# A two-layer mixer trunk: the order of projection tiles in a stage, and the evacuation of rotary tiles

## The chip, the cores and the metric

The kernel runs on one core of a Trainium2 chip. TensorE (PE in the profile) multiplies matrices into PSUM; VectorE (DVE), ScalarE (ACT) and GpSimd (POOL) do the elementwise work, and SyncE (SP) issues the DMAs. The metric is the device time of one execution in microseconds, as the median of several runs.

## The reference, cut to what matters

Two layers of a decoder trunk over 1024 positions with 1024 channels, and one final RMSNorm. Each layer normalizes x, projects it with one wide matrix, feeds three causal mixers, gates and merges their outputs, projects back and adds to x:

```python
h = rms_norm(x, norm_g) * (1.0 + scale) + shift
proj = h @ w_in
pool_u, pool_g, q, k, v, ret_g, rw, rw_g, gate_logits = jnp.split(proj, points, axis=-1)
o_pool = causal_pool_mixer(pool_u, pool_w, pool_scale) * jax.nn.silu(pool_g)
o_ret = retention(q, k, v, positions, ret_norm_g) * jax.nn.silu(ret_g)
o_rwkv = rwkv7_time_mix(rw, shift_mu, ...) * jax.nn.silu(rw_g)
branches = jnp.stack([o_pool, o_ret, o_rwkv], axis=2)
y = jnp.einsum('btnw,nwd->btnd', branches, w_branch)
merged = jnp.sum(jax.nn.sigmoid(gate_logits) * y, axis=2)
return x + gate * (merged @ w_out)
```

Retention turns q and k by position before it uses them:

```python
x1, x2 = x32[..., :half], x32[..., half:]
return jnp.concatenate([x1 * cos - x2 * sin, x1 * sin + x2 * cos], axis=-1)
```

The RWKV mixer is a recurrence over time with a state of 64x64 per head; it is the one part that cannot run over all positions at once.

## The kernel before

**Tiles.** Activations lie with channels on the 128 partitions and positions along the free axis, in two halves of 512. A projection tile is 128 output channels. Each of its two halves is accumulated over 8 blocks of input channels, with three products per block (high and low parts of weight and activation), so 48 matmuls of 128x512 for a tile. `in_tile2` (L1362) takes two of the three PSUM banks of the pool `psa` for the halves of a tile and runs half the channels into the first bank, half into the second, and then the other halves. The next tile's first half can start in the third bank; its second half needs the bank of this tile's first half, which must have been evacuated by then.

**Stages.** The work of a layer is in four stages, one for each retention head and each pair of RWKV heads. `RW(h)` (L55) stands for the three tiles k, r, v of RWKV, `RT(h)` for the four retention tiles rq, rk, rv, rg, `PL(g)` for the two pooling tiles pu, pg, and gate tiles serve as filler. `plan_layer` (L415) hands out the order, tile by tile and one ahead of the tile that runs. It looks at `prog`, the progress of the RWKV task: when that task of the current stage has reached its inversion (`prog` at 0 or more), the stage's retention tiles come, and then k, r, v of the next stage.

**Evacuation.** `evac_steps` (L1011) takes a tile out of PSUM. k, r and v go through `shift_evac` (L963): a scaled copy on ACT, and one product and sum on DVE. rq and rk go through `rotary` (L980): the table for this half, cosines over partitions 0 to 63 and sines over 64 to 127, is loaded from DRAM each time; four DVE products over 64 partitions each, and a sum on POOL. rv and pu take a copy on ACT, rg and pg a tanh on ACT and a product on DVE, a gate tile a tanh on ACT alone. A gate tile that is made early goes to DRAM and is loaded again for the merge.

**Tasks.** Work that is not projection is written as generators in five lanes ("norm", "post", "rwkv", "mix", "ada"). `pump` (L362) advances each lane after every projection matmul, by due times on the planner's own clock, and only the head of a lane runs. `evac_steps` adds `rwkv_task` (L725) when v is done, and `ret_task` (L655) or `pool_task` (L593) to "mix" when rg or pg is done. `rwkv_task` has a preparation (scans, exponentials, transposes, Gram matrices; its last DVE product is bv, L834), an inversion of small triangular blocks on DVE (L842 to L867), and 16 chunks one after another (L908). Both `ret_task` and the preparation pass their products through the two PSUM banks of tag `mx`. Retention's q, k, v and gate and pooling's inputs share eight SBUF slots (`mi`).

**Order within an engine.** The code's order is a priority; the tile framework then sets the order of each engine's instructions ahead of time, so an instruction that is ready early can stand ahead of one written before it. At run time each engine goes through its list in that order.

Of the kernel before, what the change touches and what calls it, by code (L numbers as in the profile page):

```python
# [9 lines left out]
F32 = mybir.dt.float32  # L10
# [3 lines left out]
ALU = mybir.AluOpType  # L14
# [3 lines left out]
P = 128  # L18
# [4 lines left out]
HF = 512  # L23
# [31 lines left out]
def RW(h):  # L55
    return [("k", h), ("r", h), ("v", h)]


def RT(h):
    return [("rq", h), ("rk", h), ("rv", h), ("rg", h)]  # L60


def PL(g):
    return [("pu", g), ("pg", g)]


def GT(n, *ds):
    return [("gate", n, d) for d in ds]


def BR(n, *ds):
    return [("br", n, d) for d in ds]
# [17 lines left out]
def trunk_kernel(ctx, tc, xT, cvec, pos, vecs, consts, w_ada, w_all, pool_w, lora_w, out):  # L90
    nc = tc.nc
# [10 lines left out]
    dp = ctx.enter_context(tc.tile_pool(name="dp", bufs=1, space=DRAM))  # L102
# [4 lines left out]
    def nm(s):  # L107
        uid[0] += 1
        return f"{s}_{uid[0]}"

    def slot(tag, n, w=HF):
        def f(s, dt=F32):
            return tp.tile([P, w], dt, tag=tag, name=nm(s), bufs=n)

        return f
# [4 lines left out]
    t_mi = slot("mi", 8, HF + 16)  # L120
    t_mo = slot("mo", 4, HF + 16)
    t_vp = slot("vp", 2)
    t_cs = slot("cs", 2)
    mi = lambda s: t_mi(s)[:, 0:HF]
    mo = lambda s: t_mo(s)[:, 0:HF]

# [22 lines left out]
    def cs(k, n=None):  # L149
        o = CST[k]  # L150
        return cst[:, o : o + n] if n else cst[:, o : o + 1]
# [85 lines left out]
    def run(gen):  # L237
        for _ in gen:
            pass

    rope_d = dp.tile([2, P, HF], F32, name="rope_d")

    def rope_tables():
        yield 15000
        MAGIC = 12582912.0
        TWO_PI = 2.0 * math.pi
        cw, left = [], TWO_PI
        for _ in range(3):
            e = 2.0 ** (math.frexp(left)[1] - 8)
            cw.append(math.floor(left / e) * e)  # L250
            left -= cw[-1]
        cw.append(left)
        PI_F = 3.1415925
        for h in range(2):
            s = slice(h * HF, (h + 1) * HF)
            pi = t_mo("posi", I32)[:, 0:HF]
            tc.keep_in_program_order(nc.sync.dma_start(out=pi, in_=pos[:, s].to_broadcast([P, HF])))
            ang = mo("ang")
            nc.vector.tensor_copy(ang, pi)
            nc.vector.tensor_scalar_mul(ang, ang, cs("freq"))  # L260
            n = mo("nrot")
            for big in (4096.0, 1.0):
                nc.vector.tensor_scalar(n, ang, 1.0 / (TWO_PI * big), MAGIC, op0=ALU.mult, op1=ALU.add)
                nc.vector.tensor_scalar_sub(n, n, MAGIC)
                for cc in cw:
                    nc.vector.scalar_tensor_tensor(ang, n, -cc * big, ang, op0=ALU.mult, op1=ALU.add)
                yield 6000
            m = mo("over")
            nc.vector.tensor_scalar_add(n, ang, math.pi / 2)
            nc.vector.tensor_scalar(m, n, math.pi, -TWO_PI, op0=ALU.is_gt, op1=ALU.mult)  # L270
            nc.vector.tensor_tensor(n, n, m, op=ALU.add)
            for a in (n, ang):
                nc.vector.tensor_scalar(a, a, PI_F, -PI_F, op0=ALU.min, op1=ALU.max)
            nc.scalar.activation(n[0:64, :], n[0:64, :], AF.Sin)
            nc.scalar.activation(n[64:128, :], ang[64:128, :], AF.Sin)
            nc.sync.dma_start(out=rope_d[h], in_=n)
            yield 6000

    xd = [dp.tile([8, 2, P, HF], F32, name=f"xd{l}") for l in range(1)]
# [4 lines left out]
    lanes = {k: deque() for k in names}  # L284
# [115 lines left out]
    prog = {}  # L400
    early = [set() for _ in range(L)]
# [4 lines left out]
    def out_order(l, part):  # L406
        return (2, 3, 0, 4, 5, 1, 6, 7) if kept(l) and part else range(8)
# [3 lines left out]
    def plan():  # L411
        for l in range(L):
            yield from ((l, it) for it in plan_layer(l))

    def plan_layer(l):  # L415
        yield from [("lora",)] + RW(0)
        pools = deque(PL(i) for i in range(4))
        pre = deque(GT(0, *range(8)) + GT(1, 0, 1, 4, 5, 6, 7) + GT(2, 2, 3, 4, 5, 6, 7, 0, 1) + GT(1, 2, 3))
        late = deque([("wg", 0), ("wg", 1), ("wg", 2)])
        done = 0  # L420
        while done < 4 or prog.get((l, 3), 0) < 13 or pools:
            if done < 4 and prog.get((l, done), -1) >= 0:
                yield from RT(done)
                done += 1
                if done < 4:
                    yield from RW(done)
            elif pools and 4 - len(pools) <= done and len(lanes["mix"]) < 2:
                yield from pools.popleft()
            elif pre or late:
                q = late if late and (done == 4 and prog.get((l, 3), -1) >= 0 or not pre) else pre  # L430
                it = q.popleft()
                early[l].add(it)
                yield it
            elif pools:
                yield from pools.popleft()
            elif done < 4:
                yield from RT(done)
                done += 1
                if done < 4:
                    yield from RW(done)  # L440
            else:
                break
        yield ("merge",)
        seq = GT(1, 2, 3) + BR(0, 0, 2, 4, 6) + [("wg", 0), ("wg", 1)]
        seq += GT(1, 0, 1) + BR(1, 0, 2) + GT(1, 4, 5) + BR(1, 4)
        seq += [("wg", 2), ("wg", 3)] + GT(1, 6, 7) + BR(1, 6)
        seq += GT(2, 0, 1) + BR(2, 0) + GT(2, 2, 3) + BR(2, 2) + GT(2, 4, 5, 6, 7) + BR(2, 4, 6)
        yield from [it for it in seq if it not in early[l]]
        for part in range(2 + (l + 1 == L)):
            yield from [("out", d, part) for d in out_order(l, part)]  # L450
# [41 lines left out]
    def mm1(ps, w, k, r, start, stop):  # L492
        (whi, wlo), (rh, rl) = w, r
        for j, (a, b) in enumerate(((whi, rh), (whi, rl), (wlo, rh))):
            mmul(ps, a[:, k * P : (k + 1) * P], b, start=(start and j == 0), stop=(stop and j == 2))
            pump()
# [5 lines left out]
    def acc_ps():  # L502
        return ps_a.tile([P, HF], F32, tag="acc", name=nm("acc"))
# [459 lines left out]
    def shift_evac(l, mui, ps, h, am_prev, dst):  # L963
# [13 lines left out]
        )  # L977
        return carry

    def rotary(ps, h, dst):  # L980
        cs_ = t_cs("cs")
        nc.sync.dma_start(out=cs_, in_=rope_d[h])
        cos, sin = cs_[0:64, :], cs_[64:128, :]
        lo, hi = ps[0:64, :], ps[64:128, :]
        t = mo("rot")
        nc.vector.tensor_tensor(dst[0:64, :], lo, cos, op=ALU.mult)
        nc.vector.tensor_tensor(dst[64:128, :], hi, cos, op=ALU.mult)
        nc.vector.scalar_tensor_tensor(t[0:64, :], hi, -1.0, sin, op0=ALU.mult, op1=ALU.mult)
        nc.vector.tensor_tensor(t[64:128, :], lo, sin, op=ALU.mult)  # L989
        nc.gpsimd.tensor_tensor(dst, dst, t, op=ALU.add)  # L990

    L_ = None
    pinned = [False]

    def enter_layer(l):
        nonlocal L_
        L_ = (l, {}, {}, [])
        L_[3].extend(lora_load(l))

    def lora_load(l):  # L1000
        raw = wp.tile([P, W], F32, tag="wr", name=nm("lraw"), bufs=3)
        nc.sync.dma_start(out=raw, in_=lora_w[l])
        lw = [cp.tile([P, W], F32R, tag=f"lw{j}", name=nm("lw")) for j in range(2)]
        split(raw, *lw, nc.vector)
        return lw
# [5 lines left out]
    def evac_steps(item, ps, h, bias=None):  # L1011
        l, st, ams, lw = L_
        kind = item[0]
# [65 lines left out]
    def evac(*a):  # L1079
        run(evac_steps(*a))  # L1080
# [137 lines left out]
    with tc.manual_schedule(engines={ET.PE, ET.DVE, ET.Activation, ET.Pool}):  # L1218
# [107 lines left out]
        for kt in range(8):  # L1326
            shifted(1, kt)
            mm1(pss[0, 1], first[0][1][kt // 4], kt % 4, h_cur[1][kt], kt == 0, kt == 7)
        L_ = (0, {}, {}, [])
        evac(first[0][0], pss[0, 0], 0)  # L1330
# [10 lines left out]
    run(sb)  # L1341
    L_[3].extend(lora_load(0))
    wprep()
    evac(first[0][0], pss[0, 1], 1)
    for h in range(2):
        evac(first[1][0], pss[1, h], h)
    setup_rest()
    add("mix", rope_tables())
    late_ada = [(0, g) for g in (5, 6)] + [(1, g) for g in range(7)]

    for l in range(L):
        if l:
            enter_layer(l)
# [91 lines left out]
        while wready[0][0][0] != "out":  # L1445
# [6 lines left out]
            elif it[0] == "gate":  # L1452
                n, d = it[1], it[2]
                for h, ps in enumerate(in_tile2(ws)):
                    nc.scalar.activation(gate_tile((n, d, h)), ps, AF.Tanh, scale=0.5)
            else:
                n, d0 = it[1], it[2]
# [5 lines left out]
                for d, h in dh:  # L1463
                    ps = acc_ps()
# [29 lines left out]
        for part, (h, sl) in enumerate(parts):  # L1494
# [3 lines left out]
            for i, d in enumerate(out_order(l, part)):  # L1498
# [16 lines left out]
                ps = acc_ps()[:, 0 : xr.free_size()]  # L1515
# [129 lines left out]
```

## Time and profile before

| | |
|---|---|
| median of 3 runs | 2549.88 us (2545.69 to 2555.64) |
| the profiled execution | 2560.67 us, span 2558.9 us |
| busy: PE, DVE, ACT, POOL | 95%, 55%, 31%, 33% |
| mean granted TensorE clock | 0.968 |
| table loads for rotary | 32, of 256 KB each |
| early gate halves written to DRAM | 72 |

A row of a timeline has start and length in microseconds, the engine, the line, the operation, what it writes and reads, and in brackets how long the engine sat idle before it and what ended that. A row of a group has busy time and the mean of one in ns, and then the idle time before them with its releasers. A row of windows has the window, the busy time of PE, weight loads, DVE, ACT and POOL with counts, the granted TensorE clock as a share, and the DMA share and rate. A tensor's name in such rows is that of the code, without its buffer number.

### The profile page before, as it was taken

Reading aid. Unit: us, or ns where it says so; the run is one execution under the profiler, and the core shown is the slowest. Engines: PE = TensorE matmul, PEld = TensorE weight load, DVE = VectorE, ACT = ScalarE, POOL = GpSimd, SP = SyncE. Lnnn points to the kernel's source line nnn. Section 1 sums busy time; section 2 is a strip of 40 time slices with the busy share of each in tenths; the row PEclk is TensorE's granted clock in tenths of the full one; section 3 lists DMA queues with packets and bytes.
Section 4 is the critical chain, followed back from the end, with each engine's and each line's share of the span. In section 5 each row is a group of like instructions: output and inputs, shape, how many; then the busy total and the mean of one; then the engine's idle time right before and its main releaser. Section 6 shows DMA issues by size and latency. Waiting matters only on the chain. (4 is left out here: it accounts for less than half of the span.)

```text
span 2558.9 us, 34979 instructions
## 1 busy us (share of the span) xinstructions
PE 2420.1 (95%) x13318; PEld 2000.1 (78%) x13318; DVE 1415.3 (55%) x2620; ACT 800.7 (31%) x1482; POOL 850.3 (33%) x729
## 2 busy tenths in 40 slices
PE   6888999999999899999999899999999989999998
PEld 4677887787787688777878788778778778878888
DVE  7887358257646834365464835744764583412244
ACT  4641332233133222212353223323313322222243
POOL 5422232133223223473452223223322322247341
PEclk8799999799999999999999999999999999999999
DMA  6222112112212314674540211211221121454152
GB/s 227 76 86 77 41 43 78 42 43 68 65 39 70 120 46 138 208 225 129 173 133 26 82 43 51 77 48 42 66 67 39 46 78 42 144 169 123 56 156 75
DMA packets 126329, 227.62 MB, mean 89 GB/s; under 512 B 14288, under 2 KB 17616, under 8 KB 126160
## 3 DMA queue, kind: packets, MB, share of 16 engines
q1 hardware_dynamic: 126160, 225.37, 28.2%
q8 instruction: 105, 1.72, 0.3%
q14 instruction: 64, 0.52, 0.1%
HBM read 180.75 MB, written 44.56 MB: 88 GB/s over the span
## 5 line engine op out<-in xcount | busy, mean ns | idle before, releaser
L392 PE MATMUL acc<-hhi,wh 128*128 128x512 f32 x1968 | 801.2, 407 | 53.6 <-DVE rot L989 52.0
L507 POOL TENSOR_TENSOR wl<-wr,wh 128x512 fp32r<-128x512 f32 x338 | 448.8, 1329 | 1171.9 <-ACT wh L506 1059.0
L392 PE MATMUL acc<-hlo,wh 128*128 128x512 f32 x1968 | 801.2, 407 | 0.0
L392 PE MATMUL acc<-hhi,wl 128*128 128x512 f32 x1968 | 800.8, 407 | 0.0
L392 PEld LDWEIGHTS acc<-hhi,wh 128*128 128x128 f32 x1968 | 378.1, 192 | 125.4 <-issue 55.3
L506 ACT CAST wh<-wr 128x512 fp32r<-128x512 f32 x338 | 209.4, 620 | 835.9 <-PE acc L392 658.7
L392 PEld LDWEIGHTS acc<-hlo,wh 128*128 128x128 f32 x1968 | 378.2, 192 | 73.1 <-issue 5.0
L392 PEld LDWEIGHTS acc<-hhi,wl 128*128 128x128 f32 x1968 | 377.8, 192 | 69.5 <-issue 1.1
L392 PE MATMUL acc<-olo,wh 128*128 128x512 f32 x384 | 154.7, 403 | 3.7 <-POOL olo L507 3.7
L392 PE MATMUL acc<-oG,wh 128*128 128x512 f32 x384 | 153.5, 401 | 3.1 <-DVE gs L1472 1.3
L392 PE MATMUL acc<-oG,wl 128*128 128x512 f32 x384 | 153.1, 400 | 0.0
L930 DVE SCALAR_TENSOR_TENSOR S<-ch,pc,SP 64x64 f32<-64x64 f32 x256 | 72.4, 283 | 83.8 <-PE ch L392 78.3
L916 ACT ACTIVATE SP<-S,pc 128x128 f32<-128x128 f32 x128 | 51.4, 401 | 192.5 <-DVE S L930 184.6
L852 DVE TENSOR_TENSOR tm<-MT 64x30 f32<-64x30 f32 (+14 forms) x240 | 101.8, 424 | 7.9
L1472 DVE SCALAR_TENSOR_TENSOR gs<-gs,acc 128x512 f32<-128x512 f32 x64 | 43.6, 684 | 100.6 <-PE acc L392 91.1
L858 DVE TENSOR_TENSOR MT<-MT,tm 64x30 f32<-64x30 f32 (+14 forms) x240 | 90.1, 375 | 7.9
L392 PEld LDWEIGHTS acc<-olo,wh 128*128 128x128 f32 x384 | 73.6, 192 | 22.5 <-POOL olo L507 6.4
L919 DVE TENSOR_TENSOR xst<-cy,MT 64x128 f32<-64x128 f32 x128 | 35.9, 281 | 99.8 <-PE cy L392 78.6
L392 PEld LDWEIGHTS acc<-oG,wh 128*128 128x128 f32 x384 | 73.7, 192 | 21.8 <-ACT oG L506 2.9
L925 DVE COPY Z<-ch 64x128 f32<-64x128 f32 x128 | 36.0, 281 | 94.3 <-PE ch L392 93.6
L218 DVE SCALAR_TENSOR_TENSOR ada_acc<-wada,cact,ada_acc 128x512 f32<-128x512 f32 (+1 forms) x68 | 67.3, 990 | 37.2 <-DMA wada<-in_w_ada 36.4
L392 PEld LDWEIGHTS acc<-oG,wl 128*128 128x128 f32 x384 | 73.9, 192 | 16.7
(294 smaller groups left out, 3856.7 us busy)
## 6 DMA issues: line engine op xcount, KB each, us to landing
wr<-in_w_all SPq DMA_DIRECT2D x364, 256.0 KB, 2.7
gd<-gsg SPq DMA_DIRECT2D x72, 256.0 KB, 2.0
gs<-gd SPq DMA_DIRECT2D x72, 256.0 KB, 3.0
wada<-in_w_ada SPq DMA_DIRECT2D x70, 256.0 KB, 3.1
ol<-od SPq DMA_DIRECT2D x64, 256.0 KB, 3.1
cs<-rope_d SPq DMA_DIRECT2D x32, 256.0 KB, 2.8
ringG<-in_w_ada SPq DMA_DIRECT2D x26, 256.0 KB, 5.3
x<-in_xT SPq DMA_DIRECT2D x16, 256.0 KB, 5.4
```

Source lines behind the costliest of these rows:

```text
L218: nc.vector.scalar_tensor_tensor(acc, w, cact[:, kt : kt + 1], acc, op0=ALU.mult, op1=ALU.add)
L392: nc.tensor.matmul(out, lhsT=lhsT, rhs=rhs, start=start, stop=stop, **kw)
L506: nc.scalar.copy(hi, src)
L507: eng.tensor_tensor(lo, src, hi.bitcast(F32), op=ALU.subtract)
L852: nc.vector.tensor_tensor(pr, M3[:, i + 1 :, i : i + 1].to_broadcast([64, n, i]), M3[:, i : i + 1, 0:i].to_broadcast([64, n, i]), op=ALU.mult,
L858: nc.vector.tensor_tensor(M3[:, i + 1 :, 0:i], M3[:, i + 1 :, 0:i], pr, op=ALU.add)
L916: nc.scalar.activation(SP, S, AF.Copy, scale=pcc)
L919: nc.vector.tensor_tensor(xst[0:64, :], cy[0:64, 0:P], AV[:, c * P : (c + 1) * P], op=ALU.add)
L925: nc.vector.tensor_copy(Z[0:64, c, :], ch[0:64, 0:P])
L930: nc.vector.scalar_tensor_tensor(Sn[rw, rw], ch[rw, P + 64 * hd : P + 64 * hd + 64], pc[rw, c : c + 1], SP[rw, rw], op0=ALU.mult, op1=ALU.add,
L1472: nc.vector.scalar_tensor_tensor(s, s, 1.0, ps, op0=ALU.add, op1=ALU.mult)
```

## The change

Three things are changed. In `plan_layer`, k, r, v of the next stage come ahead of the stage's retention tiles; in the last stage, where no next one exists, up to two gate tiles come there. The loop also goes on while the lane "mix" holds a task. In `rotary`, the cosines are stored twice, over all 128 partitions, so that both halves of the channels take one product; the sines of both position halves share one table. The three tables are loaded once in a layer and kept in SBUF, for which the pool `cs` gets a third slot; the tables are written to DRAM in six pieces in place of two.

```diff
-    t_cs = slot("cs", 2)
+    t_cs = slot("cs", 3)
...
-    rope_d = dp.tile([2, P, HF], F32, name="rope_d")
+    rope_d = dp.tile([3, P, HF], F32, name="rope_d")
...
-            nc.sync.dma_start(out=rope_d[h], in_=n)
+            for r in range(2):
+                nc.sync.dma_start(out=rope_d[h, 64 * r : 64 * r + 64, :], in_=n[0:64, :])
+            nc.sync.dma_start(out=rope_d[2, 64 * h : 64 * h + 64, :], in_=n[64:128, :])
...
-        while done < 4 or prog.get((l, 3), 0) < 13 or pools:
+        while done < 4 or prog.get((l, 3), 0) < 13 or pools or lanes["mix"]:
             if done < 4 and prog.get((l, done), -1) >= 0:
-                yield from RT(done)
                 done += 1
                 if done < 4:
                     yield from RW(done)
+                else:
+                    for _ in range(min(2, len(pre))):
+                        early[l].add(pre[0])
+                        yield pre.popleft()
+                yield from RT(done - 1)
...
             elif done < 4:
-                yield from RT(done)
                 done += 1
                 if done < 4:
                     yield from RW(done)
+                yield from RT(done - 1)
...
+    rope = [None, None, None]
+
     def rotary(ps, h, dst):
-        cs_ = t_cs("cs")
-        nc.sync.dma_start(out=cs_, in_=rope_d[h])
-        cos, sin = cs_[0:64, :], cs_[64:128, :]
+        for i in (h, 2):
+            if rope[i] is None:
+                rope[i] = t_cs("cs")
+                nc.sync.dma_start(out=rope[i], in_=rope_d[i])
+        sin = rope[2][64 * h : 64 * h + 64, :]
         lo, hi = ps[0:64, :], ps[64:128, :]
         t = mo("rot")
-        nc.vector.tensor_tensor(dst[0:64, :], lo, cos, op=ALU.mult)
-        nc.vector.tensor_tensor(dst[64:128, :], hi, cos, op=ALU.mult)
+        nc.vector.tensor_tensor(dst, ps, rope[h], op=ALU.mult)
         nc.vector.scalar_tensor_tensor(t[0:64, :], hi, -1.0, sin, op0=ALU.mult, op1=ALU.mult)
         nc.vector.tensor_tensor(t[64:128, :], lo, sin, op=ALU.mult)
         nc.gpsimd.tensor_tensor(dst, dst, t, op=ALU.add)
...
     def enter_layer(l):
         nonlocal L_
+        rope[:] = [None, None, None]
         L_ = (l, {}, {}, [])
```

## The prediction

> **What bounds the kernel now.** I read the page's engine row first, then the costliest groups, then who the matrix engine waits for, then the order of time around one of these waits.
>
> ```profile
> span 2558.9 us, 34979 instructions
> ...
> PE 2420.1 (95%) x13318; PEld 2000.1 (78%) x13318; DVE 1415.3 (55%) x2620; ACT 800.7 (31%) x1482; POOL 850.3 (33%) x729
> ...
> L392 PE MATMUL acc<-hhi,wh 128*128 128x512 f32 x1968 | 801.2, 407 | 53.6 <-DVE rot L989 52.0
> ```
> ```profile
> PE acc L392 <- DVE rot L989: 52.0, 8, 9.4
> ```
>
> PE is busy 95% of the span, and the change takes no matmul away. So it can only win back idle time of PE (2558.9 - 2420.1 = 138.8 us) and time at a low clock. Of the idle time 52.0 us is one wait, met eight times: a projection tile cannot start because the last rotary product (L989) has not yet freed its PSUM bank. Eight times is once per stage and layer. Here is the first of them, on PE and then on DVE:
>
> ```profile
> 239.94 0.76 PE L392 MATMUL acc<-hhi,wh 128*128 128x512 f32 x1 [7.29 <-DVE rot L989]
> ...
> 243.38 0.40 PE L392 MATMUL acc<-hhi,wl 128*128 128x512 f32 x1
> 243.61 0.40 PE L392 MATMUL acc<-hhi,wh 128*128 128x512 f32 x1
> ```
> ```profile
> 233.22 3.75 DVE L867 STREAM_TRANSPOSE G<-MT 32x1024 f32<-32x1024 f32 x2
> 237.00 0.68 DVE L986 TENSOR_TENSOR rq<-acc,cs 64x512 f32<-64x512 f32 x1
> ...
> 239.11 0.68 DVE L989 TENSOR_TENSOR rot<-acc,cs 64x512 f32<-64x512 f32 x1
> ```
>
> The stall is not the rotary alone. DVE works without a gap through the triangular inversion of `rwkv_task` (L842 to L867), and rq's evacuation stands right behind the last transpose: 237.00 is 3.75 us and a gap of 0.03 after 233.22. PE waits out the rest of the inversion and then one rotary half, 239.11 + 0.68 - 237.00 = 2.79 us. Matmuls after it run slowly for a while: eight start between 239.94 and 243.38, 0.43 us apart, against 0.23 after 243.38. At 0.23 they take 1.8 us, so a stall loses about 3.4 - 1.8 = 1.6 us more.
>
> **How long the stall is depends on when the tile arrives.** Below are the other three stages of layer 0 and the last of layer 1, and the product that stands just ahead of an inversion (bv, L834) in stages 0 to 2 of layer 0.
>
> ```profile
> 449.29 0.77 PE L392 MATMUL acc<-hhi,wh 128*128 128x512 f32 x1 [5.30 <-DVE rot L989]
> 671.20 0.76 PE L392 MATMUL acc<-hhi,wh 128*128 128x512 f32 x1 [6.17 <-DVE rot L989]
> 895.07 0.77 PE L392 MATMUL acc<-hhi,wh 128*128 128x512 f32 x1 [9.38 <-DVE rot L989]
> 2108.86 0.76 PE L392 MATMUL acc<-hhi,wh 128*128 128x512 f32 x1 [6.16 <-DVE rot L989]
> ```
> ```profile
> 203.37 0.69 DVE L834 SCALAR_TENSOR_TENSOR bv<-bon,vp 128x512 f32<-128x512 f32 x1
> ...
> 413.12 0.69 DVE L834 SCALAR_TENSOR_TENSOR bv<-bon,vp 128x512 f32<-128x512 f32 x1
> ...
> 633.88 0.64 DVE L834 SCALAR_TENSOR_TENSOR bv<-bon,vp 128x512 f32<-128x512 f32 x1
> ```
>
> From bv to the end of the stall is 36.6, 36.2 and 37.3 us in these three: nearly constant, since it is the inversion plus a rotary half. A projection tile is 48 matmuls x 0.23 = 11 us. After bv the planner finishes the tile it is in (a rest d, 0 to 11 us), then one more that it has already drawn, then rq, and a quarter of rk fits into the third bank: d + 2.25 x 11 = d + 24.75 us until PE stands still. Hence stall = 36.6 - 24.75 - d, about 12 - d, and the stalls 7.29, 5.30, 6.17 give d = 4.7, 6.7 and 5.8.
>
> **The change part by part.**
>
> ```profile
> L975 DVE SCALAR_TENSOR_TENSOR k<-acc,omu,k 128x512 f32<-128x512 f32 x14 | 10.5, 750 | 9.3 <-ACT k L967 7.7 <-ACT carry L971 0.8 <-PE ch L392 0.7
> ```
> ```profile
> L967 ACT ACTIVATE k<-acc,vec 128x511 f32<-128x511 f32 x14 | 9.6, 687 | 15.0 <-PE acc L392 14.8
> ...
> L1049 ACT ACTIVATE gsg<-acc 128x512 f32<-128x512 f32 x72 | 42.9, 595 | 53.5 <-PE acc L392 42.2 <-DVE pdl L507 8.0 <-issue 3.1
> ```
>
> (1) *Stages 0 to 2: k, r, v stand where rq stood.* k's evacuation needs ACT (687 ns, and ACT is free there) and one DVE product of 0.75 us. It waits behind the same inversion, so the stall does not go; its tail shrinks from 2.79 to 0.75, by 2.04 us. In stage 0 of either layer nothing earlier moves, so d stays: 2 x 2.04 = **-4.1 us**.
>
> (2) *Stages 1 and 2.* Here d will change, because of where the next task starts:
>
> ```profile
> 338.01 0.28 DVE L919 TENSOR_TENSOR xst<-cy,MT 64x128 f32<-64x128 f32 x1 [1.48 <-PE cy L392]
> ...
> 349.75 0.75 DVE L975 SCALAR_TENSOR_TENSOR vp<-acc,omu,vp 128x512 f32<-128x512 f32 x1 [2.22 <-POOL vp L973]
> 352.12 1.02 DVE L757 TENSOR_TENSOR_SCAN Lc<-fixed,sg 128x64 f32<-128x64 f32 x5
> ```
>
> The last of 16 chunks is at 338.0, but the next `rwkv_task` starts its scans at 352.1, just after v is there: its start, and so the tile boundary's place, is tied to v. Afterwards v comes four tiles earlier, the start is tied to the chunk end, and d may be anything from 0 to 11. With a stall of 10 - d (12 less 2.04), the mean over d is 50 / 11 = 4.5 us; the ends are 0 and 10. DVE's order is no fixed code order, though:
>
> ```profile
> 859.47 0.73 DVE L218 SCALAR_TENSOR_TENSOR ada_acc<-wada,cact,ada_acc 128x512 f32<-128x512 f32 x1
> ```
>
> A product of the ADA group, emitted much later in the code, runs between the inversion's steps. An early k may get in the same way, so I take 3.5 for 4.5. Stages 1 and 2 have 5.30 and 6.17 now, mean 5.74: 4 x (3.5 - 5.74) = **-9.0 us**, bounds 4 x -5.74 = -23 and 4 x (10 - 5.74) = +17.
>
> (3) *Stage 3.* No k follows, so two gate tiles stand there. They are evacuated by ACT alone (595 ns), and retention's tiles come 22 us later, after the inversion. Both stalls go: -(9.38 + 6.16) = **-15.5 us**, and with them two slow restarts, 2 x 1.6 = **-3.2 us**. What is late next: rq's products then meet chunk steps of 0.28 us, inside the 5.5 us (half a tile) that a bank may take.
>
> (4) *Three products, tables in SBUF.* The one 128x512 product is nearest to bv's, also 128x512 with one side in PSUM, 0.69 us: as long as one of 64 rows (0.68). So a rotary half falls from 2.79 to about 2.1, and 32 x 0.69 = 22 us of DVE go. After (1) no rotary stands on PE's path, so I count **0**; if an early retention tile met a busy DVE, it would be worth 0.7 each, 22 us at most. 26 table loads go:
>
> ```profile
> cs<-rope_d SPq DMA_DIRECT2D x32, 256.0 KB, 2.8
> ```
>
> The page's waits have none of PE or DVE for them. Four more table writes go out while the tables are made, which is done before the rotary at 237.00 now and so before a later one. The first rotary of a layer waits for two loads (2.8 us), and behind it on DVE stand chunk steps; the load can issue as soon as the table and a slot are there. Bounds: 0 to 2 x 2.8.
>
> (5) *What moves along.* k, r, v's weight loads on SP, their weight splits on ACT and POOL and POOL's carry copies go four tiles earlier; retention's weights, splits and rotary sums on POOL (33% busy) go three tiles later. Equal counts cross each queue: 0. The loop now also runs while a mixer task is left; that turns gate tiles into early ones, with a write to DRAM and a load by SP, which none of PE's waits names: 0.
>
> (6) *Retention's task now runs beside the next task's preparation* rather than beside the chunks. That is the unpaid cost. PE's waits in stage 3's preparation (786 to 870 us), which has a pooling task and the previous chunk's tail beside it, and the two rows for slots:
>
> ```profile
> PE pps L392 <- ACT pdh L506: 2.7, 2, 1.4
> PE bt L398 <- DVE BK L789: 2.7, 1, 2.7
> PE yt L398 <- POOL yc L652: 0.9, 1, 0.9
> ```
> ```profile
> L392 PE MATMUL rs<-rq,rk x128: 270/275/275, 291.6 to 2182.6; 128*128 128x128 f32 x128
> ```
> ```profile
> L392 PE MATMUL ro<-R,rq x112: 275/275/275, 301.7 to 2191.6; 128*128 128x128 f32 x112
> ```
>
> Another companion may cost as much as pooling's, 2.7 + 2.7 + 0.9 = 6.3 us, in six preparations (stages 1 to 3 twice): 0 to +38. Pooling's first tile also follows retention's last directly and needs one of the eight `mi` slots, all held by retention until rq's last read, 301.7 - 291.6 = 10 us after its start: about one tile, so just hidden. I take 1 us per preparation, **+6**: the planner delays such steps until their inputs are modelled as ready, and only few slip.
>
> Sum: -4.1 - 9.0 - 15.5 - 3.2 + 6 = **-25.8 us**. The profiled execution took 2560.7 us, so 2534.9. It is itself 10.8 above the median of 2549.9, and the windows say why:
>
> ```profile
> 458.00:482.00 24.00, 24.00 (x155) 18.20 (x156) 4.74 (x7) 4.66 (x8) 2.55 (x2) 0.51 0.07 18
> 1687.00:1711.00 24.00, 24.00 (x234) 19.54 (x232) 7.78 (x16) 5.94 (x12) 5.12 (x4) 1.00 0.19 52
> ```
>
> After the second stall PE had half its clock for 24 us (24 x 0.49 = 11.8 us lost); at the same place of layer 1 it had all of it. The medians need not hold this, so from the median: 2549.9 - 25.8 = **2524 us**. The Trainium skill, "TensorE: Matmul & The Clock Gate", section "What's actually happening", says that half rate ends after one busy window of about 3.4 us. By it the first row could not be, with PE busy 24.0 of 24.0 us; the measurement decides. By the rule, a removed stall saves at most 1.7 us of clock, an estimate; by the row, one stall in eight costs 11.8, another 1.5 us each, and the sum would be some 3 us more.
>
> **The rivals.** *All stalls go* (20%): k arrives late enough, or gets in between the inversion's steps, everywhere. Then -52.0 - 8 x 1.6 + 6 = -58.8, 2491 us. For it: a late d suffices, and 859.47. Against it: stage 0 keeps its d. *The stall is handed on* (20%): k arrives early and waits nearly 10 us in stages 1 and 2: -4.1 + 17 - 15.5 - 3.2 + 6 = 0, 2550 us. For it: in all eight places the evacuation stood behind the whole inversion. *Preparation chokes* (10%), slower: retention and preparation share the two `mx` PSUM banks, and PE stands in order behind a transpose (bt, nps) whose bank is late. At 6.3 us in six preparations, each with a slow restart of 1.6, +47 against -31.8: 2565 us. It decides from 31.8 / 6 = 5.3 us per preparation. Against it: at its present place retention's task causes PE hardly any wait. That the order does not change is excluded, the planner writes it out.
>
> **How the numbers follow.** My forecast holds 50%, alone 2508 to 2540. The range takes in the first rival's time, the second's and part of the third: 2490 to 2556. A measurement tells about 0.5% (12.7 us) from no change: faster 0.68 (48 of the 50 and the 20), same 0.22, slower 0.10.
>
> **What would show it.** Right: the wait of PE on L989 is gone, one on k's product (L975) of 3 to 5 us stands in stages 0 to 2, none in stage 3; DVE busy some 22 us less; scans of the next task begin within 5 us of the last chunk. Wrong: PE waits on bt, nps, rs or pps that sum to 30 us more than before, or a wait on L975 as long as L989's was.

## The result and the profile after

The changed kernel takes 2536.07 us (median of 9 runs, 2523.59 to 2544.02), the kernel before 2557.56 in its 9 runs (2545.69 to 2564.63). The ratio is 0.9919, with a 95% interval of 0.989 to 0.9949: about 21 us or 0.8% less. The profiled execution took 2538.03 us, against 2560.67 before. The page of the changed kernel, the rows that answer to those shown of before (L394 is before's L392, L981 its L975):

```profile
span 2536.3 us, 34936 instructions
...
PE 2417.6 (95%) x13318; PEld 1995.5 (79%) x13318; DVE 1394.0 (55%) x2588; ACT 796.6 (31%) x1482; POOL 847.6 (33%) x729
...
L394 PE MATMUL acc<-hhi,wh 128*128 128x512 f32 x1968 | 799.5, 406 | 29.1 <-DVE k L981 29.1
```

The matmuls are the same 13318, so the span splits into PE's busy time and its idle time. Busy: 2420.1 to 2417.6, -2.5 us (the mean granted clock is 0.968 before and 0.971 now). Idle: 138.8 to 2536.3 - 2417.6 = 118.7, **-20.1 us**. So nearly the whole gain is idle time. DVE lost 21.3 us of work, which by itself is no time of PE. Who PE now waits for (us in total, times, longest):

```profile
PE acc L394 <- DVE k L981: 29.1, 6, 6.4
...
PE rot L400 <- DVE yc L658: 8.7, 6, 2.1
...
PE acc L394 <- POOL olo L513: 5.8, 5, 2.0
```

The wait for the last rotary product, 52.0 us in eight, is gone, and a wait for k's product stands there: 29.1 us in six. PE's timeline has all six, one for each of stages 0 to 2 of either layer:

```profile
237.30 0.80 PE L394 MATMUL acc<-hhi,wh 128*128 128x512 f32 x1 [6.12 <-DVE k L981]
...
452.61 0.79 PE L394 MATMUL acc<-hhi,wh 128*128 128x512 f32 x1 [5.74 <-DVE k L981]
...
666.17 0.80 PE L394 MATMUL acc<-hhi,wh 128*128 128x512 f32 x1 [6.36 <-DVE k L981]
...
1448.18 0.80 PE L394 MATMUL acc<-hhi,wh 128*128 128x512 f32 x1 [4.05 <-DVE k L981]
...
1647.15 0.80 PE L394 MATMUL acc<-hhi,wh 128*128 128x512 f32 x1 [4.26 <-DVE k L981]
...
1863.69 0.80 PE L394 MATMUL acc<-hhi,wh 128*128 128x512 f32 x1 [2.56 <-DVE k L981]
```

VectorE's timeline ahead of the first, and VectorE and ScalarE in stage 3 of layer 0 (two fences, as they are two answers):

```profile
232.71 3.75 DVE L873 STREAM_TRANSPOSE G<-MT 32x1024 f32<-32x1024 f32 x2
236.49 1.41 DVE L981 SCALAR_TENSOR_TENSOR k<-acc,omu,k 128x512 f32<-128x512 f32 x2
...
883.39 3.93 DVE L873 STREAM_TRANSPOSE G<-MT 32x1024 f32<-32x1024 f32 x2
```
```profile
883.55 0.60 ACT L1059 ACTIVATE gsg<-acc 128x512 f32<-128x512 f32 x1 [2.28 <-PE acc L394]
888.06 0.60 ACT L1059 ACTIVATE gsg<-acc 128x512 f32<-128x512 f32 x1
```

The picture is before's, with one thing exchanged. k's product starts at 236.49, right after the last transpose, as rq's did; PE goes on at 237.30, after one such product in place of a whole rotary half. In stage 3 a gate tile is taken out by ScalarE at 883.55, while VectorE is still at its transposes, and PE has no wait there.

### The profile page after: what moved, and what is told of

Its sections match the earlier page's. It is cut to its first block, busy times and chain, and to the rows that moved or that the text cites. A ratio compares the mean times of both kernels' runs of the same rounds, so it can differ in the third digit from the quotient of the medians.

```text
span 2536.3 us, 34936 instructions
## 1 busy us (share of the span) xinstructions
PE 2417.6 (95%) x13318; PEld 1995.5 (79%) x13318; DVE 1394.0 (55%) x2588; ACT 796.6 (31%) x1482; POOL 847.6 (33%) x729
## 5 line engine op out<-in xcount | busy, mean ns | idle before, releaser
L394 PE MATMUL acc<-hhi,wh 128*128 128x512 f32 x1968 | 799.5, 406 | 29.1 <-DVE k L981 29.1
L394 PE MATMUL acc<-hlo,wh 128*128 128x512 f32 x1968 | 801.7, 407 | 0.0
L394 PE MATMUL acc<-hhi,wl 128*128 128x512 f32 x1968 | 799.2, 406 | 0.0
L394 PEld LDWEIGHTS acc<-hhi,wh 128*128 128x128 f32 x1968 | 377.7, 192 | 100.4 <-DVE k L981 31.6
L394 PEld LDWEIGHTS acc<-hhi,wl 128*128 128x128 f32 x1968 | 377.6, 192 | 68.8 <-issue 2.2
L394 PEld LDWEIGHTS acc<-hlo,wh 128*128 128x128 f32 x1968 | 377.2, 192 | 68.8 <-issue 1.3
L394 PE MATMUL acc<-olo,wh 128*128 128x512 f32 x384 | 154.2, 402 | 5.8 <-POOL olo L513 5.8
L394 PE MATMUL acc<-oG,wh 128*128 128x512 f32 x384 | 153.1, 400 | 3.5 <-ACT oG L512 1.7
L394 PE MATMUL acc<-oG,wl 128*128 128x512 f32 x384 | 152.5, 398 | 0.0
L864 DVE TENSOR_TENSOR MT<-MT,tm 64x30 f32<-64x30 f32 (+14 forms) x240 | 95.2, 397 | 7.8
L394 PEld LDWEIGHTS acc<-olo,wh 128*128 128x128 f32 x384 | 73.2, 191 | 24.6 <-POOL olo L513 8.9
L394 PEld LDWEIGHTS acc<-oG,wh 128*128 128x128 f32 x384 | 73.2, 191 | 22.7 <-ACT oG L512 2.9
L394 PEld LDWEIGHTS acc<-oG,wl 128*128 128x128 f32 x384 | 73.6, 192 | 16.6
```

The costliest lines, as they stand in the source:

```text
L394: nc.tensor.matmul(out, lhsT=lhsT, rhs=rhs, start=start, stop=stop, **kw)
L864: nc.vector.tensor_tensor(M3[:, i + 1 :, 0:i], M3[:, i + 1 :, 0:i], pr, op=ALU.add)
```

## The experiments

Eleven more runs were made, one of them (e_after) of the changed kernel again. All are timed against the kernel before; the ratio sets a run against the executions of before that were made beside it. "Stall" is PE's wait for the product of k or of the rotary that stands behind the inversion, "merge" is its wait for `olo`, the low part that POOL makes for the merge, "early" counts gate halves written to DRAM. Busy, idle and clock are those of PE in the profiled execution, which is one of several and need not be the typical one: e_gate1's is its slowest, e_order's its fastest.

| kernel | median us | ratio (95%) | busy | idle | clock | stall | merge | early |
|---|---|---|---|---|---|---|---|---|
| kernel before | 2557.56 | 1 | 2420.1 | 138.8 | 0.968 | 52.0 | 3.7 | 72 |
| changed kernel | 2536.07 | 0.9919 (0.9890-0.9949) | 2417.6 | 118.7 | 0.971 | 29.1 | 5.8 | 80 |
| e_after (the same again) | 2528.73 | 0.9893 (0.9854-0.9932) | 2410.5 | 114.5 | 0.974 | 29.2 | 5.8 | 80 |
| e_order | 2542.72 | 0.9948 (0.9922-0.9974) | 2412.4 | 121.1 | 0.977 | 24.5 | 7.5 | 80 |
| e_rotary | 2546.33 | 0.9969 (0.9945-0.9993) | 2414.6 | 131.7 | 0.972 | 44.1 | 4.7 | 72 |
| e_nogates | 2544.01 | 0.9953 (0.9929-0.9976) | 2428.1 | 121.9 | 0.966 | 35.1 | 4.1 | 72 |
| e_gate1 | 2531.78 | 0.9899 (0.9859-0.9939) | 2447.0 | 99.4 | 0.960 | 5.2 | 6.5 | 78 |
| e_gate2 | 2540.17 | 0.9959 (0.9938-0.9980) | 2428.6 | 117.5 | 0.966 | 0 | 3.8 | 76 |
| e_spread | 2562.11 | 1.0030 (1.0013-1.0047) | 2418.9 | 135.4 | 0.972 | 24.1 | 19.3 | 94 |
| e_gate2_spread | 2530.47 | 0.9913 (0.9891-0.9934) | 2412.9 | 115.8 | 0.976 | 0 | 18.8 | 94 |
| e_oldgate | 2536.50 | 0.9939 (0.9917-0.9960) | 2408.6 | 117.0 | 0.973 | 9.9 | 17.0 | 96 |
| e_rv | 2507.39 | 0.9806 (0.9764-0.9847) | 2415.8 | 89.3 | 0.972 | 3.8 | 3.9 | 76 |
| e_rv_spread | 2503.78 | 0.9789 (0.9752-0.9826) | 2404.3 | 99.8 | 0.980 | 0 | 9.7 | 84 |

**The theory**: PE stands still because the tile behind the inversion needs VectorE to leave PSUM. Whatever stands there inherits the stall; the change shortens its tail in stages 0 to 2 and ends it in stage 3. **The rivals**: the rotary made shorter is what helps, not the order; or a stall that is taken away comes back elsewhere.

**Each part alone.** e_order is the kernel before with the new order and the old rotary; e_rotary is the changed kernel with the old order. The main part of what e_order changes in the kernel before (the loop's condition and the second branch change as in the whole change):

```diff
...
-                yield from RT(done)
                 done += 1
                 if done < 4:
                     yield from RW(done)
+                else:
+                    for _ in range(min(2, len(pre))):
+                        early[l].add(pre[0])
+                        yield pre.popleft()
+                yield from RT(done - 1)
...
```

> The new order with the old rotary (four products, a table load for each half). Theory (what PE loses is its wait for whatever VectorE evacuates right after the inversion): as the changed kernel, 0.992 of before within 0.003; PE waits on k's product about 29 us in six places, none on a rotary product. Rival (the shorter rotary and its kept tables carry the gain): 0.997 or more, waits on a rotary product in the trace.

> The old order with the new rotary. Theory: the eight waits stay and each loses only the fourth product, 0.69 us: 52 to about 46 us, 0.998 of before, within what can be told from no change. Rival (the rotary carries the gain): 0.995 or less, and waits of half the length.

The waits of e_order and, below, of e_rotary:

```profile
PE acc L392 <- DVE k L979: 24.5, 6, 6.0
```
```profile
PE acc L394 <- DVE rot L994: 44.1, 8, 7.2
```

With the order alone the rotary's wait is gone and k's six stand there. With the rotary alone all eight rotary waits are left, each about one VectorE product shorter: 52.0 - 44.1 = 7.9 us, 1.0 each; three products in place of four take 0.7 off. So the order does the exchange, and the rotary cuts a tail. The ratios multiply to 0.9948 x 0.9969 = 0.9917, the changed kernel's own. That looks like two gains that add, but e_after's interval overlaps that of e_order, and with the new order no rotary stands on PE's path; whether the rotary still brings anything there is not settled.

**Stage 3 without its gates.** e_nogates takes the two gate tiles out again:

```diff
-                else:
-                    for _ in range(min(2, len(pre))):
-                        early[l].add(pre[0])
-                        yield pre.popleft()
```

> The changed kernel without the two gate tiles in stage 3, so retention's tiles follow the inversion there. Theory: the two waits of stage 3 come back, 5 to 9 us each less 0.69, and two slow restarts: 10 to 20 us above the changed kernel, 0.996 to 1.0 of before. Rival (stage 3 gained by the order or by the shorter rotary, not by the gates): as the changed kernel, 0.992.

```profile
PE acc L394 <- DVE k L977: 29.1, 6, 6.4
...
PE acc L394 <- DVE rot L994: 6.0, 1, 6.0
```

A rotary wait comes back, in layer 0 alone. So the gates take away 6.0 of the 15.5 us that stage 3 lost; the stall of layer 1 is gone even without them, and what in the moved work removed it is not shown. The median, 2544.01 against 2536.07, points the same way, with intervals that overlap; its ratio of 0.9953 lies a little below the 0.996 to 1.0 that was forecast.

**A gate tile in every stage.** e_gate1 puts one gate tile ahead of k in stages 0 to 2, e_gate2 two in every stage (N is 1 or 2; stage 3 keeps its two):

```diff
             if done < 4 and prog.get((l, done), -1) >= 0:
+                for _ in range(min(N if done < 4 else 2, len(pre))):
+                    early[l].add(pre[0])
+                    yield pre.popleft()
                 done += 1
                 if done < 4:
                     yield from RW(done)
-                else:
-                    ...
                 yield from RT(done - 1)
```

> The changed kernel with one early gate tile ahead of k in stages 0 to 2 as well. Theory (wait = 10 - d, and a gate adds 11 to d): the six waits on k's product go, 29 us, and six slow restarts of 1.6: some 39 us below the changed kernel, 0.977 of before. Rival (the wait moves to the next tile with a product on VectorE, or into the preparation): waits of 20 us or more on other tiles, 0.988 or more.

> Two early gate tiles ahead of k in every stage. One was enough for most of the waits (29 us became 5), so by the theory the rest goes: no wait on k's product, idle time 4 to 5 us below that with one. The clock is what limits now (mean 0.969 with one gate): 0.988 to 0.991 of before. Rival (the waits went to other places): idle time of PE not below that with one gate.

The waits of e_gate1, then those of e_gate2:

```profile
PE acc L394 <- DVE k L980: 5.2, 2, 3.2
```
```profile
PE rot L400 <- DVE yc L657: 20.0, 12, 2.9
...
PE pps L394 <- ACT MT L884: 8.2, 2, 4.2
```

One gate does what the theory says: the stall falls from 29.1 to 5.2 us and PE's idle time by 19.3. But the time did not follow: 0.9899 where 0.977 was forecast, with an interval that overlaps the changed kernel's. PE's *busy* time in this profile is 29.4 us longer than the changed kernel's, for the same matmuls, at a clock of 0.960. (It is the slowest of its six runs, 2548.18; the others are 2520 to 2534. Where runs of both kernels have the same mean clock, e_gate1's is about 10 us shorter: 2533.69 against 2544.02 at 0.966, 2522.02 against 2531.70 at 0.974.) The windows show one place (us from the start, PE busy with count, then weight loads, VectorE, ScalarE, POOL, the granted clock, DMA share and rate), and PE's timeline what stands ahead of it:

```profile
449.60:473.50 23.90, 23.90 (x155) 18.14 (x154) 0.00 (x0) 4.38 (x8) 1.28 (x1) 0.50 0.02 6
```
```profile
446.08 1.19 PE L394 MATMUL m<-MT,G 32*32 32x32 f32 x32
...
448.09 1.19 PE L394 MATMUL m<-MT,G 32*32 32x32 f32 x32
449.22 0.51 PE L394 MATMUL acc<-hlo,wh 128*128 128x512 f32 x1
449.55 0.60 PE L394 MATMUL acc<-hhi,wl 128*128 128x512 f32 x1
```

PE is busy for all of 23.90 us at half its clock, without a gap before, and the stretch begins as the 32x32 matmuls that join the inverted blocks run through. That is 12 us lost in one place, and the trace has three more, of 23.9, 27.3 and 34.1 us. In e_gate2 its rival holds, and the time, 0.9959, misses the 0.988 to 0.991 of the theory: no stall is left, and other waits take its place, 20.0 us in twelve for retention's output (`rot` on PE, `yc` on VectorE) and 8.2 at the pooling product, so that the idle time is that of the changed kernel.

**The small matmuls spread out.** If the clock falls because small matmuls come packed, a longer due time between their groups should keep it. e_spread does that to the changed kernel, e_gate2_spread to e_gate2 (the first of the two changed lines stands twice, once for each of the groups m1 and m2):

```diff
                 if u % 16 == 15:
-                    yield 600
+                    yield 2600
...
             nc.scalar.copy(AV[:, q * HF : (q + 1) * HF], ps[0:64, :])
-            yield 400
+            yield 2600
```

> The changed kernel with the three groups of small matmuls behind the inversion (m1 and m2 of 32x32, av of 64x64) spread out: 2.6 us of planner time between groups in place of 0.4 to 0.6. Theory (stretches of 17 us and more at half clock come from these small matmuls standing close together): no such stretch in the stages, mean clock 0.977 or more against 0.9726, some 8 us below the changed kernel, 0.988 to 0.990 of before, waits on k's product unchanged at about 29 us. Rival (the stretches follow from the waits, or are chance): stretches and clock as in the changed kernel, 0.992.

> Both: two gate tiles ahead of k in every stage, and the small matmuls spread out. Theory: neither wait nor long stretch: 0.980 to 0.984 of before, clock 0.980 or more. Rival (the two are one effect): as the better of the two alone, 0.988.

Half right. In e_gate2, long stretches in three stages become none, the busy time falls by 15.7 us, all five runs have a clock of 0.976 or 0.977 (0.964 to 0.975 without), and they lie within 2529.67 to 2532.74, where they had been 2531.72 to 2556.71. In the changed kernel the clock did not rise: its profile had one long stretch in the stages (23.9 us at 2078.6) and e_spread's has none, yet its mean clock is 0.972 where 0.977 was forecast, and the busy time stays (2417.6 and 2418.9). Both times miss their forecasts, and e_gate2_spread's 0.9913 is no better than the changed kernel's 0.9919. One reason is that the stages are longer. The place of e_spread that answers to 666.17 comes at 691.02; more gate tiles are drawn to fill the time (94 halves early), and the merge pays:

```profile
691.02 0.79 PE L394 MATMUL acc<-hhi,wh 128*128 128x512 f32 x1 [3.72 <-DVE k L981]
```
```profile
PE acc L394 <- POOL olo L513: 19.3, 19, 2.7
```

At 2.6 us a group this costs the changed kernel more than it brings (1.003).

**The old order with gates.** e_oldgate puts two gates ahead of retention's tiles in the kernel before, with the old rotary:

```diff
             if done < 4 and prog.get((l, done), -1) >= 0:
+                for _ in range(min(2, len(pre))):
+                    early[l].add(pre[0])
+                    yield pre.popleft()
                 yield from RT(done)
```

> The kernel before with nothing but two early gate tiles ahead of retention's in every stage: old order, old rotary. Theory (only what stands in the slot behind the inversion counts, not which tiles change places): all eight waits on a rotary product go, 52 us, 0.985 to 0.990 of before, as with two gates in the new order. Rival (the new order is needed): a wait on a rotary product remains, 0.995 or more.

```profile
PE acc L392 <- POOL olo L510: 17.0, 16, 3.0
PE acc L392 <- ACT oG L509: 16.5, 5, 12.4
PE acc L392 <- DVE rot L992: 9.9, 1, 9.9
```

The rotary's stall falls from 52.0 to 9.9 us with k, r, v where they were. So neither the new order nor the new rotary is needed for it; what is needed is a tile that VectorE needn't take out. The time, 0.9939, misses the 0.985 to 0.990 of the theory, and one of the eight waits is left. The price is in the merge: all 96 gate halves are spent early, and the merge waits 17.0 + 16.5 = 33.5 us for its splits, 12.4 of them in one wait. In the table the merge's wait goes with the early halves: 3.8 to 7.5 us at 72 to 80, 9.7 at 84, 17.0 to 19.3 at 94 to 96. No run sets that number alone, so the link is seen, not isolated.

**A tile that costs no gate.** rv is evacuated by a copy on ScalarE and has to be made anyway. e_rv puts it behind the inversion, then k, r, v of the next stage (one gate in the last), then rq, rk, rg; e_rv_spread adds due times of 1500 (1.5 us) between the small groups. e_rv against the changed kernel:

```diff
                 done += 1
+                rq, rk, rv, rg = RT(done - 1)
+                yield rv
                 if done < 4:
                     yield from RW(done)
                 else:
-                    for _ in range(min(2, len(pre))):
+                    for _ in range(min(1, len(pre))):
                         early[l].add(pre[0])
                         yield pre.popleft()
-                yield from RT(done - 1)
+                yield from (rq, rk, rg)
```

> The changed kernel once more, beside the next two: 0.992 of before within 0.003, so that the new order with the old rotary (0.9948) can be set against a second measurement of both parts together. If the rotary adds nothing once the order is new, 0.995; if the two add up, 0.992.

> In every stage retention's rv, which ACT alone evacuates, stands behind the inversion in place of a gate tile, then k, r, v of the next stage (in the last stage one gate tile), then rq, rk, rg. Theory (one tile without a VectorE product is enough, and gate tiles are a stock that the merge needs): waits on k as with one gate tile, 0 to 8 us in all, 80 or fewer early gate halves, waits on olo in the merge not above 7 us; 0.985 to 0.990 of before. Rival (the clock takes it back, since small matmuls then start their low stretches anyway): idle time as forecast, mean clock 0.970 or less, 0.990 or more.

> The same, with 1.5 us of planner time between the groups of small matmuls (2.6 us kept the stretches away but made each stage some 17 us longer and used up the gate tiles). Theory: no stretch of 17 us at half clock in the stages, some 88 early gate halves or fewer, clock 0.975 or more, 0.983 to 0.988 of before. Rival (the longer stage costs the merge what the clock gains): as without it.

Waits of e_rv, and its ScalarE and VectorE in stage 0:

```profile
PE rot L400 <- DVE yc L660: 3.9, 3, 2.4
PE acc L394 <- DVE k L983: 3.8, 1, 3.8
```
```profile
223.45 0.59 ACT L1089 COPY rv<-acc 128x512 f32<-128x512 f32 x1 [2.28 <-PE acc L394]
```
```profile
230.44 4.03 DVE L875 STREAM_TRANSPOSE G<-MT 32x1024 f32<-32x1024 f32 x2
235.20 0.75 DVE L983 SCALAR_TENSOR_TENSOR k<-acc,omu,k 128x512 f32<-128x512 f32 x1 [0.74 <-ACT carry L979]
```

rv leaves PSUM while VectorE still inverts, and k comes when VectorE has been free for 0.74 us. One stall of 3.8 us is left of six, and of the early gate halves there are 76. This is more than was expected of e_rv: 0.9806, and 2507.39 against e_after's 2528.73 beside it, 0.8% less. Against the changed kernel's profile the idle time falls by 118.7 - 89.3 = 29.4 us: 25.3 of the stall, 4.8 at retention's output, 1.9 in the merge, the rest in small change both ways. e_rv_spread has the highest clock of all, 0.980, and runs within 4.1 us of each other (e_rv: 9.2), but pays some of it back at the merge and at `bt`; its ratio of 0.9789 is not distinguishable from e_rv's. Both beat the changed kernel.

## Why the prediction was right, and where it was not

The forecast was 2524 us, 25.8 less than before; measured were 21 less, on a median of before that itself moved from 2549.9 to 2557.6 with more runs. In the profiled executions it was 2560.67 to 2538.03, 22.6 less, where 2534.9 had been forecast. Term by term these 22.6 are: stalls of stages 0 to 2, 7.4 where 13.1 were forecast; stalls of stage 3, 15.5 as forecast; PE's busy time, 2.5 for the 3.2 of the restarts; waits in mixers and preparation, +5.2 for +6; and another 2.4 less that no term had (waits in the chunks alone, `cy` and `ch`, go from 3.9 us to none). That the sum came so near is in part luck: what (2) fell short was partly made up by waits that the prediction did not count.

- **The bound was read rightly.** The gain is PE's idle time, and within it the wait behind the inversion. e_gate1, e_oldgate and e_rv remove most of that wait (29.1 to 5.2, 52.0 to 9.9, 29.1 to 3.8 us), in two orders and with two kinds of tile that ScalarE evacuates.
- **(1) Stage 0: the tail confirmed.** Predicted were two stalls of 2.04 us less, with k behind the same inversion. In layer 0 the stall goes from 7.29 to 6.12 us, in layer 1 from 6.17 to 4.05, together 3.3 us of the 4.1. In layer 0 the tail shrank as forecast (last transpose to PE's next matmul: 2.97 us before, 0.84 now), but PE reached the stall 1.5 us earlier, so "d stays" did not quite hold. The row of before in layer 1:

```profile
1469.47 0.77 PE L392 MATMUL acc<-hhi,wh 128*128 128x512 f32 x1 [6.17 <-DVE rot L989]
```

- **(2) Stages 1 and 2: the direction right, the size less than half, the reason wrong.** 14 us of stall were forecast in four places, 9.0 less than before; 5.74 + 6.36 + 4.26 + 2.56 = 18.9 came, 4.1 less. The step that failed is "its start, and so the tile boundary's place, is tied to v. Afterwards v comes four tiles earlier, the start is tied to the chunk end". VectorE's timeline of the changed kernel (v's last product, the last chunk, the first scan of the next task, in stages 0 and 1):

```profile
273.78 0.75 DVE L981 SCALAR_TENSOR_TENSOR vp<-acc,omu,vp 128x512 f32<-128x512 f32 x1 [0.34 <-ACT vp L973]
...
332.69 0.28 DVE L925 TENSOR_TENSOR xst<-cy,MT 64x128 f32<-64x128 f32 x1 [0.72 <-PE cy L394]
...
342.09 0.69 DVE L759 TENSOR_TENSOR ksl<-ksq,ksh 128x512 fp32r<-128x512 f32 x1 [0.99 <-ACT ksh L757]
345.61 1.54 DVE L763 TENSOR_TENSOR_SCAN Lc<-fixed,sg 128x64 f32<-128x64 f32 x3 [2.83 <-PE yt L400]
```
```profile
548.82 0.28 DVE L925 TENSOR_TENSOR xst<-cy,MT 64x128 f32<-64x128 f32 x1
...
560.24 1.57 DVE L763 TENSOR_TENSOR_SCAN Lc<-fixed,sg 128x64 f32<-128x64 f32 x8
```

At the last chunk v has been there for 59 us, and the scans still start 12.9 and 11.4 us after the last chunk; before it was 352.12 - 338.01 = 14.1. Between the two stands work of the task's own: its last output's norm, and the norm of k (`ksl`). Untied from v, the scans came only 1.2 us sooner behind the chunk in stage 0, so v, which ended 2 us before them in the kernel before, was hardly what held them. The sign "within 5 us of the last chunk" was therefore wrong. The range of 0 to 10 us for each stall held, and the value taken in it was 1.2 us too low. Of the sign "3 to 5 us" for each of the six waits only two are inside, 4.05 and 4.26.

- **(3) Stage 3: the term held, not all of its cause.** Both stalls went, 15.5 us, as forecast. Without the gates 6.0 us come back, not 15.5. The slow restarts were to give 3.2; PE's busy time fell by 2.5, which doesn't isolate them: each of the two profiles also holds one stretch of 23.9 us at half clock (458.3 us before, 2078.6 now), and that these two cancel is luck. The prediction put the first of them down to the stall at 449.29; the windows show the clock back at 0.99 from 454.80 to 458.30 and then 0.50, so that stretch is not the restart of that stall.
- **(4) The rotary: 0 on the path, not refuted.** VectorE lost 21.3 us of the 22 forecast. In the old order, where the rotary did stand on PE's path, it is worth 7.9 us of stall.
- **(5) Moves, 0:** no wait of PE names a weight, a table or a slot in either list.
- **(6) Retention beside the preparation: +6 forecast.** PE's waits in mixers and preparation (`rot`, `bt`, `nps`, `pps`, `yt`, `g` and what is smaller) sum to 32.1 us before and 37.3 now, +5.2. The sum hides an exchange, which the groups show, before and then after:

```profile
L398 PE MATMUL bt<-cst,BK 128*128 128x128 f32 x128 | 20.5, 286 | 14.7 <-DVE BK L789 10.6 <-DVE po L629 3.6 <-ACT BKt L813 0.5
...
L398 PE MATMUL rot<-cst,yc 128*128 128x128 f32 x64 | 9.9, 273 | 0.0
```
```profile
L400 PE MATMUL bt<-cst,BK 128*128 128x128 f32 x128 | 19.2, 274 | 3.3 <-DVE BK L795 2.7 <-ACT BKt L819 0.5
...
L400 PE MATMUL rot<-cst,yc 128*128 128x128 f32 x64 | 10.5, 289 | 8.7 <-DVE yc L658 8.7
```

Retention's last transposes, which never waited, now wait 8.7 us beside the preparation, while `bt`, which had waited 14.7, waits 3.3. *Preparation chokes* is the rival that this rules out here; in e_gate2, with two gates more, the same wait grows to 20.0. *All stalls go* did not happen: six waits on k's product are left. *The stall is handed on* holds for its mechanism (k stands where rq stood, and PE waits for it) but not for its price.

## What to carry to other kernels

When PE waits for a bank behind a long run of work on VectorE, ask first which engine empties the bank: a tile that another engine can evacuate, put in that slot, ends most of the wait, where other tiles of the same engine only shorten its tail. Take for it a tile that has to be made anyway at that point, not filler from a limited stock that a later phase lives on. And read busy time and granted clock beside idle time: in e_gate1 19.3 us of idle time went, and in its profile the busy time of the same matmuls grew by 29.4 us at a clock of 0.960.

## What was not expected of the hardware

Half the clock for 24 us and longer, with PE busy all or nearly all the time, is no accident of one run. The row of before at 458 us shows it, e_gate1 has it in four of its eight stages, and e_rv in two, here in one of them:

```profile
643.60:667.50 23.90, 23.90 (x155) 18.12 (x154) 1.50 (x2) 5.29 (x10) 1.49 (x3) 0.50 0.04 12
```
```profile
640.13 1.19 PE L394 MATMUL m<-MT,G 32*32 32x32 f32 x32
...
642.15 1.19 PE L394 MATMUL m<-MT,G 32*32 32x32 f32 x32
...
643.61 0.63 PE L394 MATMUL acc<-hhi,wl 128*128 128x512 f32 x1
```

Again it begins right behind two groups of 32 matmuls of 32x32 within 3.2 us. Such groups alone do not decide it. The ten profiled executions without spreading have 80 stages, nearly all with the first two groups 2.0 us apart, and only 14 have a stretch of 17 us or more at half clock around the groups (four in e_gate1, none in e_after, e_order and e_oldgate). Two of the longest begin ahead of the first group, at a stall: 34.1 us in e_gate1 from 1869.5 and 30.7 us in e_rv from 1831.4, with stalls that end at 1870.44 and 1829.93. With the groups spread out, none of the 24 stages of three executions has one, and in e_rv_spread the same work has the full clock. (Ahead of the first stage and between the layers there are stretches of up to 20.5 us in these kernels too, but there PE is idle for part of the time: in e_spread it is busy for 13.52 of the 20.50 us from 76.20.) Below are the 40 us from the first such group of this stage on, of e_rv and then of e_rv_spread, with its two first groups, now 2.9 us apart:

```profile
640.00:680.00 40.00, 39.91 (x295) 31.88 (x295) 6.16 (x16) 10.75 (x21) 3.32 (x6) 0.70 0.07 21
```
```profile
660.00:700.00 40.00, 40.00 (x339) 32.48 (x338) 7.46 (x16) 13.52 (x26) 6.20 (x9) 1.00 0.12 34
```
```profile
660.97 1.19 PE L394 MATMUL m<-MT,G 32*32 32x32 f32 x32
...
663.90 1.19 PE L394 MATMUL m<-MT,G 32*32 32x32 f32 x32
```

So within the stages the long stretches were seen only where small matmuls are packed, though not at most such places, and PE counts as busy in them. What in them does it, and why it lasts 24 to 34 us at one time and is absent at the same place in another run, no run here shows. The Trainium skill, "TensorE: Matmul & The Clock Gate", section "What's actually happening", has half rate follow an idle window and end after one busy window of about 3.4 us; the rows with PE busy for 23.90 of 23.90 us at 0.50 disagree with both, as far as busy in the rows is what the section means by it, and the measurement decides. The time of a run also goes with its clock: the nine of the changed kernel go from 2523.59 us at a mean clock of 0.979 to 2544.02 at 0.966.
